# Laying the operand tiles of a decoder layer at one address residue, and cutting the key and value columns at 256

## The chip, the cores and the metric

The kernel runs on one core of a Trainium2 chip. The metric is the device time of one execution in microseconds; less is better. Its operands are float32; most matrix products are made from a high and a low part of each operand, in three matmuls (high by high, high by low, low by high).

## The reference

One decoder layer over 1024 tokens of width 1024 (batch 1), cut to its lines of computation:

```python
mod = silu(c) @ ada_w + ada_b                       # six rows: shift, scale, gate, twice
u = rms_norm(h, norm1_g) * (1 + scale1) + shift1
z = u @ w_in                                        # queries, keys, values, gates, 2 x 1024 merge columns
y_a = nsa_attention(...) @ w_up_nsa                 # compressed, selected and window branches, 8 heads
y_b = stick_breaking_attention(q_b, k_b, v_b) @ w_up_sb
mixed = (sigmoid(m_a) * y_a + sigmoid(m_b) * y_b) @ w_out
h = h + gate1 * mixed
u2 = rms_norm(h, norm2_g) * (1 + scale2) + shift2
h = h + gate2 * (square(relu(u2 @ mlp_w1)) @ mlp_w2)    # 4096 hidden columns
```

## The kernel before

The program is one straight list of work in stages. The times are those of the profiled execution.

- 0 to 185 us: normalisation, modulation, the first projections. `block_mm` (L302, L306) and `q_mm` (L577) make queries and the sources of the compressed blocks; `kv_mm` (L588) makes keys, values and gates for each of 8 token tiles, in two groups of 24 matmuls, over columns 0 to 272 and 272 to 536.
- to 600 us: `nsa_all`, the sparse attention. Logits are two matmuls a chunk (L825, L826: query tile `qh` or `ql` as weights, `kT` streamed); the probabilities are turned (L943) and multiplied with the values (L909: `vS` as weights, `th` or `tl` streamed). In between, `drive` and `pump` put 1,344 matmuls of `unit_mm` (L746) that project the remaining 28 blocks of 128 columns of `w_in` (weights `uwh`, `uwl`; `uh`, `ul` streamed, 512 columns each).
- to 880 us: `sb_gens`, the stick-breaking attention, with the rest of `unit_mm` in between.
- to 975 us: `up_unit`, 16 units for each of two branches, 12 matmuls a unit (L1324: weights `wh`, `wl`; the attention outputs `oh`, `ol` streamed). Branch 0 runs three units ahead: the first three units are of branch 0 alone, then the branches alternate, and the last three are of branch 1 alone.
- to 1105 us: `out_mm`, 16 units of 24 matmuls (L1428: `mth`, `mtl` as weights, `wh` or `wl` streamed), and the second normalisation with its turns (L1447).
- to the end: the channel mixer in 8 chunks of 512 hidden columns. `hidden_units` is 8 units a chunk of 24 matmuls (L1512: `wh`, `wl` as weights, `mth`, `mtl` streamed, which by then hold `u2`); `product` is 7 products a chunk of 24 matmuls (L1561: `rah`, `ral` as weights, `wbh`, `wbl` streamed). One unit and one product take turns, until the last chunk, whose seven products have no further units beside them.

"Weights" is the 128 x 128 operand that TensorE loads, "streamed" the operand of up to 512 columns that runs past it; the loading of the next weights overlaps the running matmul.

Tiles come from two stacks of pools that grow from either end of the on-chip memory, "left" from below and "right" from above. A pool's place is what the pools opened before it leave. Each tile takes its size rounded up to 32 bytes, so that a pool with odd-sized tiles shifts all that is opened after it. What is given below as a residue is a tile's start within a partition, modulo 512 bytes, as the built program has it:

| pool (side) | tiles | before | after |
|---|---|---|---|
| uT, wu, mt, ml (left) | uh, ul, uwh, uwl, mth, mtl, rah, ral, wbh, wbl | 128 | 128 |
| p1a (left) | wh1, wl1 (2176 bytes each, 8 buffers) | 0, 128, 256, 384 | the same |
| xt (right) | xT, xa, ch1, cl1 | 448 | 128 |
| kv (right) | kT, vS, kcT | 192 | 128 |
| at (right) | qh, ql | 384 | 128 |
| at (right) | Sn, Pn, Pf | 128 | 128 |
| at (right) | th, tl | 448 | 128 |
| sb (right) | Q, Kh, Kl, V | 64 | 128 |
| sb (right) | th, tl, sigr | 448 | 128 |
| wr, wx, wq (right) | raw, wh, wl | 448 | 128 |
| ya (right) | oh, ol of branch 0 | 448 | 128 |
| yb (left) | oh, ol of branch 1 | 128 | 128 |

A weight or streamed slice starts at its tile's residue plus a multiple of 512, but for the slices of `wh1` and `wl1` in `kv_mm`: the first group starts at the tile's residue, the second 272 x 4 = 1088 bytes behind it, which is 64 more modulo 128.

Of the kernel before, what the change touches and what calls it, by code (L numbers as in the profile page):

```python
# [6 lines left out]
F32 = mybir.dt.float32  # L7
# [10 lines left out]
NT = 8  # L18
# [17 lines left out]
def build(tc, I, out):  # L36
# [89 lines left out]
    pre_l = pre.tile([128, NK, 128], F32R, name="uwl")  # L126
    p1a = pool("p1a", "left")

    pool("odd", "right").tile([128, 8], F32, name="odd")
    xt_pool = pool("xt", "right")  # L130


# [263 lines left out]
    kvp = pool("kv", "right")  # L396
    kT = kvp.tile([128, 4, S], F32R, name="kT")
    vS = kvp.tile([128, NT, 4, 2, HD], F32R, name="vS")
    kcT = kvp.tile([128, 2, HD], F32R, name="kcT")
    gates = kvp.tile([128, NT, 8, 3], F32, name="gates")  # L400
    vC = kvp.tile([HD, 2, 2, HD], F32R, name="vC")
    bnp = pool("bn", "right")
    Bn = bnp.tile([128, 8, 256], F32, name="Bn")
# [177 lines left out]

    def kv_mm(t):
        raw = pb.tile([128, 544], F32, name="kvr", bufs=2)
        for c, (c0, c1) in enumerate(((0, 272), (272, 536))):
            p = (pd, psx)[c]()
            for k in range(NK):
                for n, (a, b) in enumerate(three(k, slice(t * 128, (t + 1) * 128))):
                    nc.tensor.matmul(p[:, :c1 - c0], a, ws[k][b][:, c0:c1],  # L588
                                     start=(k == 0 and n == 0), stop=(k == NK - 1 and n == 2))
            nc.scalar.copy(raw[:, c0:c1], p[:, :c1 - c0])  # L590
        return raw
# [59 lines left out]
    for n, (kind, t) in enumerate(jobs):  # L651
# [8 lines left out]
        if kind == "q":  # L660
            b = q_mm(t)
# [6 lines left out]
        else:  # L668
            if t == 0:
                ws = wk  # L670
            b = kv_mm(t)
# [86 lines left out]
    at = pool("at", "right")  # L758
# [43 lines left out]

    PT_ = 0.216


    def nsa_a(i, kv, hp, qT, P):
        n0, n1 = max(0, i - 1), i + 1
        x0 = 256 - (n1 - n0) * 128
        nb = 8 * i + 8
        chunks = plan(i)  # L810
        ngm = at.tile([128, 2, 2, 3], F32, name="ngm", bufs=2)
        sms = at.tile([128, 2, 2, 3], F32, name="sms", bufs=2)
        if len(chunks) < 6:
            nc.vector.memset(ngm, 3e38)
            nc.vector.memset(sms, 0.0)
        late = None
        for g in range(2):
            h = kv * 4 + hp * 2 + g
            q0, q1 = qT[0][:, hp * 2 + g], qT[1][:, hp * 2 + g]
            for br, c, a, b in chunks:  # L820
                n = (b - a) * 128
                p = psx()
                em = br == 1 and c == 1 and i >= 4
                kk = kT[:, br * 2 + kv, a * 128:b * 128]
                track(nc.tensor.matmul(p[:, :n], q0, kk, start=True, stop=False))  # L825
                track(nc.tensor.matmul(p[:, :n], q1, kk, start=False, stop=not em))  # L826
                if em:
                    track(nc.tensor.matmul(p[:, :128], identr, edger, start=False, stop=True))
                nm = ngm[:, br, g, c:c + 1]
                sm = sms[:, br, g, c:c + 1]  # L830
                if c == 0:
                    src = at.tile([128, 256], F32, name="Sn", bufs=3)
                    nc.vector.tensor_tensor_reduce(src[:, :n], p[:, :n], Bn[:, h, x0:], -1.0, 3e38,
                                                   op0=OP.add, op1=OP.min, accum_out=nm)
                    dst = at.tile([128, 256], F32, name="Pn", bufs=8)
                else:
                    src = p
                    nc.vector.tensor_reduce(nm, p[:, :n], axis=AX.X, op=OP.max, negate=True)
                    dst = at.tile([128, 384], F32, name="Pf", bufs=12)
                P[br, g, c] = dst  # L840
                if late:
                    late()

                def late(src=src, dst=dst, n=n, c=c, nm=nm, sm=sm):
                    nc.scalar.activation(dst[:, :n], src[:, :n], AF.Exp, scale=-1.0 if c == 0 else 1.0,
                                         bias=nm, accum_out=sm)
                yield max(n, 256) * 2 / 2400.

        p = psx()
        for g in range(2):  # L850
            for q in range(2):
                track(nc.tensor.matmul(p[:, g * 64:g * 64 + nb], qT[q][:, hp * 2 + g], kcT[:, kv, :nb],
                                 start=q == 0, stop=q == 1))
        late()
        sc = at.tile([128, 2, HD], F32, name="sc", bufs=2)
        nc.vector.tensor_tensor(sc[:, :, :nb], p[:, :128].rearrange("p (g c) -> p g c", g=2)[:, :, :nb],
                                Bc[:, kv * 4 + hp * 2:kv * 4 + hp * 2 + 2, 56 - 8 * i:56 - 8 * i + nb], op=OP.add)
        mc = at.tile([128, 2], F32, name="mc", bufs=2)
        nc.vector.tensor_reduce(mc, sc[:, :, :nb], axis=AX.X, op=OP.max, negate=True)
        nc.vector.scalar_tensor_tensor(sc[:, :, :nb], mc[:, :, None].to_broadcast([128, 2, nb]), 1e20, sc[:, :, :nb],  # L860
                                       op0=OP.min, op1=OP.add)
        pcx = at.tile([128, 2, HD], F32, name="pcx", bufs=2)
        P["c"] = pcx

        mm = at.tile([128, 2, 2], F32, name="mm", bufs=2)
        nc.vector.tensor_reduce(mm, ngm, axis=AX.X, op=OP.min)
        fc = at.tile([128, 2, 2, 3], F32, name="fc", bufs=2)
        nc.vector.tensor_tensor(fc, mm[:, :, :, None].to_broadcast([128, 2, 2, 3]), ngm, op=OP.subtract)
        yield 0.43
        nc.scalar.activation(pcx[:, :, :nb], sc[:, :, :nb], AF.Exp)  # L870
        nc.scalar.activation(fc, fc, AF.Exp)
        yield 0.0
        tot = at.tile([128, 3, 2], F32, name="tot", bufs=2)
        nc.vector.tensor_reduce(tot[:, 0], pcx[:, :, :nb], axis=AX.X, op=OP.add)
        nc.vector.tensor_tensor(sms, sms, fc, op=OP.mult)
        nc.vector.tensor_reduce(tot[:, 1:3], sms, axis=AX.X, op=OP.add)
        nc.vector.tensor_scalar(tot, tot, 1e-30, None, op0=OP.max)
        nc.vector.reciprocal(tot, tot)
        h0 = kv * 4 + hp * 2
        nc.vector.tensor_tensor(tot, tot, gates[:, i, h0:h0 + 2].rearrange("p g s -> p s g"), op=OP.mult)  # L880
        nc.vector.tensor_tensor(fc, fc, tot[:, 1:3][:, :, :, None].to_broadcast([128, 2, 2, 3]), op=OP.mult)
        nc.gpsimd.tensor_tensor(pcx[:, :, :nb], pcx[:, :, :nb], tot[:, 0][:, :, None].to_broadcast([128, 2, nb]), op=OP.mult)
        P["fc"] = fc
        yield 0.0


    def nsa_b(i, kv, hp, P):
# [42 lines left out]
        for n in range(len(items) + 2):  # L930
# [3 lines left out]
            if n <= last:  # L934
                it = items[n]
                p = pt()
# [17 lines left out]
            yield cost  # L954
        tmp = at.tile([64, 256], F32, name="otmp", bufs=2)
        nc.scalar.copy(tmp, po_[64:128, :256])
        o = at.tile([64, 256], F32, name="osum", bufs=2)
        nc.vector.tensor_tensor(o, po_[0:64, :256], tmp, op=OP.add)
        h0 = (kv * 4 + hp * 2) * HD
        nc.sync.dma_start(oa_d[h0:h0 + 128, i * 128:(i + 1) * 128].rearrange("(g d) q -> d g q", g=2),  # L960
# [93 lines left out]


    def sb_gens(sp):
        zero = sp.tile([128, 16], F32, name="zero")[:, 0:1]
        nc.vector.memset(zero, 0.0)

        def load(u, h):  # L1060
# [54 lines left out]
        def sb_a(kind, chunk, ops, A, edges):  # L1115

            i, c0, c1 = chunk
            Q, Kh, Kl = ops
            w = c1 - c0
            p = psx()  # L1120
            qs = Q[:, i * 128:(i + 1) * 128]
            diag = kind != 2
            track(nc.tensor.matmul(p[:, :w], qs, Kh[:, c0:c1], start=True, stop=False))
            track(nc.tensor.matmul(p[:, :w], qs, Kl[:, c0:c1], start=False, stop=not diag))
            if diag:
                track(nc.tensor.matmul(p[:, w - 128:w], identr, diagr, start=False, stop=True))
            sig = sp.tile([128, w], F32, name="sigr" if kind == 1 else "sig%d" % w, bufs=5 if kind == 1 else 2)
            nc.scalar.activation(sig, p[:, :w], AF.Sigmoid, scale=HD ** -0.5)
            nc.scalar.activation(p[:, :w], p[:, :w], AF.Sigmoid, scale=-(HD ** -0.5))
            A[i, kind] = (sig, c0)  # L1130

            def fin():
                Pt = sp.tile([128, 528], F32, name="Pt", bufs=6)
                if diag:
                    nc.vector.memset(Pt[:, w:w + 1], 1.0)
                else:
                    nc.vector.tensor_copy(Pt[:, w:w + 1], edges.pop(i)[:, 0:1])
                nc.vector.tensor_tensor_scan(Pt[:, 0:w][:, ::-1], p[:, 0:w][:, ::-1], zero.to_broadcast([128, w]),
                                             1.0 if diag else Pt[:, w:w + 1], op0=OP.mult, op1=OP.add)
                nc.gpsimd.tensor_tensor(sig, sig, Pt[:, 1:w + 1], op=OP.mult)  # L1140
                if kind == 1:
                    edges[i] = Pt
            return fin, max(w, 256) * 2 / 2400.
# [469 lines left out]
```

## Time and profile before

| | |
|---|---|
| median of three runs | 1754.13 us (1746.5 to 1754.78) |
| the profiled execution | 1753.26 us |
| its span, first to last instruction | 1751.5 us |
| TensorE (PE) busy | 1694.7 us, 97% |
| weight loads (PEld) | 1414.9 us, 81% |
| VectorE (DVE) | 1141.8 us, 65% |
| ScalarE (ACT) | 819.8 us, 47% |
| GpSimd (POOL) | 876.1 us, 50% |
| mean granted clock of TensorE | 0.989 |

The profile is of one execution. A busy share says how long some instruction of an engine was under way; matmuls overlap each other (one that is shown with 0.39 us may start 0.23 us after the one before), so the pace of TensorE is read from the starts, not from the durations.

### The profile page before, as it was taken

To read this page: it belongs to the slowest core of one execution; us is meant where nothing else is said; L and a number is where in the kernel's file an instruction comes from. 1 tells how busy PE (TensorE), PEld (TensorE's weight loads), DVE (VectorE), ACT (ScalarE), POOL (GpSimd) and SP (SyncE) were. 2 spreads that over 40 slices of the span, in tenths; PEclk is the share of its full clock that TensorE was granted. 3 is DMA by queue.
4 is the path that set the end of the run, shared out by engine and by line. 5 is a ranking of instruction groups with operands and counts; after the bars stand their busy time and mean duration, and the time that the engine had idled before them with its cause. 6 is when DMAs were issued, how large, how long until landed. Compare 5 with 4: busy or idle time off the path is not lost.

```text
span 1751.5 us, 25194 instructions
## 1 busy us (share of the span) xinstructions
PE 1694.7 (97%) x8652; PEld 1414.9 (81%) x8652; DVE 1141.8 (65%) x2514; ACT 819.8 (47%) x1809; POOL 876.1 (50%) x824
## 2 busy tenths in 40 slices
PE   5999999999999989999999899999999999999998
PEld 4879888888888867788778688888888888888886
DVE  7597478778777567878464564365656575756458
ACT  6433476666666466766433244333333333333332
POOL 0021143434333387865164400786857675858676
PEclk8999999999999989999999999999999999999999
DMA  9365311111121264531485611121212020202102
GB/s 304 97 185 160 109 46 55 55 54 54 49 61 38 62 167 124 157 88 46 135 256 183 216 37 73 38 71 37 70 39 73 25 73 25 72 25 72 41 21 97
DMA packets 153656, 157.14 MB, mean 90 GB/s; under 512 B 13544, under 2 KB 117688, under 8 KB 153528
## 3 DMA queue, kind: packets, MB, share of 16 engines
q1 hardware_dynamic: 149304, 153.42, 29.3%
q10 hardware_dynamic: 4224, 2.10, 0.4%
q8 instruction: 69, 1.13, 0.3%
q14 instruction: 59, 0.48, 0.1%
HBM read 128.21 MB, written 27.28 MB: 89 GB/s over the span
## 4 chain that ended last, share of the span: by engine, by line
PE 83%; DMA 5%; DVE 4%; POOL 3%; ACT 3%; issue 2%; SPq 1%; POOLq 0%; DVEq 0%; ACTq 0%
PE px L1512 20%; PE px L1561 16%; PE pd L746 15%; PE px L1428 5%; PE po L909 4%; PE pt L943 4%; PE px L1324 3%; DMA adraw<-in_ada_w_dram 2%; PE psx L825 2%; PE psx L826 2%; PE cb L302 1%; PE pd L588 1%; PE po L1175 1%; PE psx L588 1%; PE pt L1155 1%
## 5 line engine op out<-in xcount | busy, mean ns | idle before, releaser
L1564 DVE TENSOR_TENSOR acc<-acc,px 128x512 f32<-128x512 f32 x384 | 243.9, 683 | 119.8 <-PE px L1561 114.5
L1512 PE MATMUL px<-mtl,wh 128*128 128x512 f32 x512 | 202.9, 396 | 0.0
L1512 PE MATMUL px<-mth,wl 128*128 128x512 f32 x512 | 202.7, 396 | 0.0
L1512 PE MATMUL px<-mth,wh 128*128 128x512 f32 x512 | 202.5, 396 | 0.0
L746 PE MATMUL pd<-uh,uwh 128*128 128x512 f32 x448 | 181.3, 405 | 0.7 <-ACT zo L1018 0.7
L1561 PE MATMUL px<-wbl,rah 128*128 128x512 f32 x448 | 175.3, 391 | 2.2 <-POOL wbl L1537 1.9
L746 PE MATMUL pd<-ul,uwh 128*128 128x512 f32 x448 | 177.1, 395 | 0.0
L746 PE MATMUL pd<-uh,uwl 128*128 128x512 f32 x448 | 177.1, 395 | 0.0
L1561 PE MATMUL px<-wbh,ral 128*128 128x512 f32 x448 | 174.9, 390 | 0.0
L66 DVE TENSOR_TENSOR wl<-raw,wh 128x1024 fp32r<-128x1024 f32 x48 | 76.3, 1591 | 149.1 <-ACT wh L61 128.7
L1561 PE MATMUL px<-wbh,rah 128*128 128x512 f32 x448 | 172.1, 389 | 0.0
L1537 POOL TENSOR_TENSOR wbl<-raw,wbh 128x1024 fp32r<-128x1024 f32 x40 | 106.0, 2649 | 91.9 <-ACT wbh L1536 91.6
L1523 POOL TENSOR_TENSOR w<-w,grow 128x1024 f32<-128x1024 f32 x32 | 82.8, 2602 | 97.0 <-DVE grow L1296 96.4
L901 DVE TENSOR_TENSOR tl<-pt,th 128x512 fp32r<-128x512 f32 (+8 forms) x168 | 103.7, 620 | 34.3 <-ACT th L900 33.0
L1535 POOL TENSOR_TENSOR raw<-r 128x512 f32<-128x512 f32 x80 | 109.9, 1397 | 20.0 <-DVE wl L66 17.9
L900 ACT CAST th<-pt 128x512 fp32r<-128x512 f32 (+8 forms) x168 | 88.8, 531 | 60.6 <-PE pt L943 58.0
L1512 PEld LDWEIGHTS px<-mth,wl 128*128 128x128 f32 x512 | 96.2, 188 | 23.6 <-issue 0.5
L1512 PEld LDWEIGHTS px<-mtl,wh 128*128 128x128 f32 x512 | 96.3, 188 | 23.0 <-issue 0.2
L1512 PEld LDWEIGHTS px<-mth,wh 128*128 128x128 f32 x512 | 96.2, 188 | 22.9 <-issue 0.2
L1536 ACT CAST rah<-raw 128x1024 fp32r<-128x1024 f32 x40 | 42.1, 1052 | 153.1 <-PE px L1561 139.7
L1561 PEld LDWEIGHTS px<-wbl,rah 128*128 128x128 f32 x448 | 84.1, 188 | 22.1 <-POOL wbl L1537 3.1
L746 PEld LDWEIGHTS pd<-uh,uwl 128*128 128x128 f32 x448 | 84.7, 189 | 18.1
(322 smaller groups left out, 4548.3 us busy)
## 6 DMA issues: line engine op xcount, KB each, us to landing
raw<-in_mlp_w_dram SPq DMA_DIRECT2D x32, 512.0 KB, 4.0
w<-in_mlp_w_dram SPq DMA_DIRECT2D x32, 512.0 KB, 4.0
z_d<-zo SPq DMA_DIRECT2D x56, 256.0 KB, 2.2
uwr<-in_w_in_dram SPq DMA_DIRECT2D x54, 256.0 KB, 3.0
adraw<-in_ada_w_dram SPq DMA_DIRECT2D x48, 256.0 KB, 2.9
xa<-in_ada_w_dram SPq DMA_DIRECT2D x32, 256.0 KB, 6.1
zr<-z_d SPq DMA_DIRECT2D x32, 256.0 KB, 4.8
m<-z_d SPq DMA_DIRECT2D x32, 256.0 KB, 3.6
```

The costliest lines, as they stand in the source:

```text
L66: (nc.vector if e == "v" else nc.gpsimd).tensor_tensor(dst, src, f(h), op=OP.subtract)
L746: r = nc.tensor.matmul(p, a, b, start=(k == 0 and n == 0), stop=(k == NK - 1 and n == 2))
L900: nc.scalar.copy(th[:rows, :w], p[:rows, :w])
L901: nc.vector.tensor_tensor(tl[:rows, :w], p[:rows, :w], f(th)[:rows, :w], op=OP.subtract)
L909: track(nc.tensor.matmul(po_[:, :256], w, tt[q][:rows, m * 256:(m + 1) * 256], start=(n == 0 and m == 0 and q == 0), stop=(n == last and m ...
L1428: nc.tensor.matmul(p, a[:, k, ts_], b[:, k % 2], start=(k == 0 and n == 0), stop=(k == NK - 1 and n == 2))
L1512: nc.tensor.matmul(p, a[:, k], b[th][:, k], start=(k == 0 and m == 0), stop=(k == NK - 1 and m == 2))
L1523: nc.gpsimd.tensor_tensor(t, t, grow2, op=OP.mult)
L1535: nc.gpsimd.tensor_tensor(d, block(i0, j0, s), block(i1, j1, s), op=OP.add if sg > 0 else OP.subtract)
L1537: (nc.vector if e == "v" else nc.gpsimd).tensor_tensor(l.rearrange("p s n -> p (s n)"), src, f(h).rearrange("p s n -> p (s n)"), op=OP.sub ...
L1561: nc.tensor.matmul(p, a[:, s, qs], b[:, s], start=(s == 0 and n == 0), stop=(s == 1 and n == 2))
L1564: nc.vector.tensor_tensor(acc[:, t, ds_], acc[:, t, ds_], p, op=OP.add if sg > 0 else OP.subtract)
```

## The change

Six paddings. The tile `odd`, which nothing reads, grows from 8 to 88 columns and so moves everything on the right by 320 bytes. `gates` (768 bytes) takes 1024. The small tiles of `nsa_a` (48, 24, 16 or 8 bytes) take 256 bytes each; `osum` takes 1152 for 1024; `zero` takes 512 for 64; `Pt` 2560 for 2112. And `kv_mm` cuts its 536 columns at 256 instead of 272.

```diff
-    pool("odd", "right").tile([128, 8], F32, name="odd")
+    pool("odd", "right").tile([128, 88], F32, name="odd")
...
-    gates = kvp.tile([128, NT, 8, 3], F32, name="gates")
+    gates = kvp.tile([128, 256], F32, name="gates")[:, :NT * 24].rearrange("p (t h s) -> p t h s", t=NT, h=8)
...
-        for c, (c0, c1) in enumerate(((0, 272), (272, 536))):
+        for c, (c0, c1) in enumerate(((0, 256), (256, 536))):
...
+    def small(name, n=12):
+        return at.tile([128, 64], F32, name=name, bufs=2)[:, :n]
...
-        ngm = at.tile([128, 2, 2, 3], F32, name="ngm", bufs=2)
-        sms = at.tile([128, 2, 2, 3], F32, name="sms", bufs=2)
+        ngm, sms = (small(n).rearrange("p (b g c) -> p b g c", b=2, g=2) for n in ("ngm", "sms"))
...
-        mc = at.tile([128, 2], F32, name="mc", bufs=2)
+        mc = small("mc", 2)
...
-        mm = at.tile([128, 2, 2], F32, name="mm", bufs=2)
+        mm = small("mm", 4).rearrange("p (b g) -> p b g", b=2)
...
-        fc = at.tile([128, 2, 2, 3], F32, name="fc", bufs=2)
+        fc = small("fc").rearrange("p (b g c) -> p b g c", b=2, g=2)
...
-        tot = at.tile([128, 3, 2], F32, name="tot", bufs=2)
+        tot = small("tot", 6).rearrange("p (b g) -> p b g", b=3)
...
-        o = at.tile([64, 256], F32, name="osum", bufs=2)
+
+        o = at.tile([64, 288], F32, name="osum", bufs=2)[:, :256]
...
-        zero = sp.tile([128, 16], F32, name="zero")[:, 0:1]
+        zero = sp.tile([128, 128], F32, name="zero")[:, 0:1]
...
-                Pt = sp.tile([128, 528], F32, name="Pt", bufs=6)
+                Pt = sp.tile([128, 640], F32, name="Pt", bufs=6)
```

The order of the instructions stays as it was on POOL and SP; on PE, DVE and ACT a few neighbours in the stretch of `kv_mm` and of the compressed blocks change places. On PE, in the first keys and values tile, these rows stand before (`wh` and `wl` are the weights' high and low columns of `w_in`, numbered by buffer; `uh`, `ul` the tokens; `pd` and `psx` the two output banks):

```order
L588 MATMUL pd<-wh_1128,uh 128x272
L588 MATMUL pd<-wl_1129,uh 128x272
L588 MATMUL pd<-wh_1128,ul 128x272
L588 MATMUL psx<-wh_1116,uh 128x264
L588 MATMUL psx<-wl_1117,uh 128x264
L588 MATMUL pd<-wh_1134,uh 128x272
```

and these in their place now:

```order
L588 MATMUL pd<-wh_1128,uh 128x256
L588 MATMUL pd<-wl_1129,uh 128x256
L588 MATMUL pd<-wh_1128,ul 128x256
L588 MATMUL psx<-wh_1116,uh 128x280
L588 MATMUL psx<-wl_1117,uh 128x280
L588 MATMUL pd<-wh_1134,uh 128x256
```

The number of matmuls and the sum of the columns are the same; 16 columns have moved from the first group to the second.

Where a new pool is laid over an old one, what its tiles wait for follows their addresses. On SP's queue, at the start of `up_unit`, the loads of the attention outputs (`raw`) and of the merge columns (`m`) stand before as

```order
L1309 DMA raw<-oa_d 128x1024 [waits DMAHW3_49,Pool_49]
L1329 DMA m_11387<-z_d 128x512 [waits DMAHW4_49]
L1329 DMA m_11559<-z_d 128x512 [waits DMAHW5_49,PE_49]
L1329 DMA m_11580<-z_d 128x512 [waits DMAHW6_49]
L1329 DMA m_11607<-z_d 128x512 [waits DMAHW7_49]
```

and now as

```order
L1312 DMA raw<-oa_d 128x1024 [waits DMAHW3_49,Pool_49]
L1332 DMA m_11387<-z_d 128x512 [waits DMAHW4_49]
L1332 DMA m_11559<-z_d 128x512 [waits DMAHW5_49]
L1332 DMA m_11580<-z_d 128x512 [waits DMAHW6_49,PE_49]
L1332 DMA m_11607<-z_d 128x512 [waits DMAHW7_49]
```

The wait for TensorE has moved from the second load of `m` to the third. On the new kernel's lines all numbers behind L802 are 2 or 3 higher: L1512 is L1515 there, L1561 is L1564, L1324 is L1327, L1428 is L1431.

## Rows read from the trace of the kernel before

**Rows 1.** The page's chain that ended last, by line.
```profile
PE px L1512 20%; PE px L1561 16%; PE pd L746 15%; PE px L1428 5%; PE po L909 4%; PE pt L943 4%; PE px L1324 3%; DMA adraw<-in_ada_w_dram 2%; PE psx L825 2%; PE psx L826 2%; PE cb L302 1%; PE pd L588 1%; PE po L1175 1%; PE psx L588 1%; PE pt L1155 1%
```
**Rows 2.** Busy us by stage: window, its length, engines' busy (instructions), clock, DMA.
```profile
160.00:600.00 440.00, 436.49 (x2808) 386.97 (x2806) 323.08 (x1172) 268.79 (x820) 157.07 (x318) 1.00 0.21 58
600.00:880.00 280.00, 262.14 (x1370) 216.72 (x1369) 193.01 (x363) 173.15 (x387) 166.60 (x171) 0.98 0.43 120
880.00:990.00 110.00, 103.50 (x452) 83.41 (x451) 58.81 (x68) 40.81 (x64) 60.33 (x42) 0.97 0.61 196
990.00:1105.00 115.00, 114.55 (x529) 93.44 (x528) 59.07 (x109) 47.48 (x119) 5.25 (x5) 1.00 0.28 101
1105.00:1751.50 646.50, 640.59 (x2773) 520.24 (x2771) 390.06 (x482) 214.78 (x290) 469.74 (x264) 1.00 0.17 52
```
**Rows 3.** Page's groups: count, busy us, mean ns, idle before and its releaser.
```profile
L1512 PE MATMUL px<-mtl,wh 128*128 128x512 f32 x512 | 202.9, 396 | 0.0
...
L1561 PE MATMUL px<-wbl,rah 128*128 128x512 f32 x448 | 175.3, 391 | 2.2 <-POOL wbl L1537 1.9
```
**Rows 4.** Timeline of PE in the last chunk: start us, duration us, line, operands.
```profile
1704.42 0.39 PE L1512 MATMUL px<-mth,wl 128*128 128x512 f32 x1
...
1706.05 0.39 PE L1561 MATMUL px<-wbh,rah 128*128 128x512 f32 x1
...
1707.44 0.39 PE L1561 MATMUL px<-wbh,rah 128*128 128x512 f32 x1
...
1716.96 1.07 PE L1561 MATMUL px<-wbh,rah 128*128 128x512 f32 x4
```
**Rows 5.** Timeline of PE, L1324 while branch 0 runs alone.
```profile
883.57 0.39 PE L1324 MATMUL px<-oh,wh 128*128 128x512 f32 x1
...
887.42 0.39 PE L1324 MATMUL px<-ol,wh 128*128 128x512 f32 x1
```
**Rows 6.** Timeline of PE, L1324 while branch 1 runs alone.
```profile
966.03 0.39 PE L1324 MATMUL px<-oh,wl 128*128 128x512 f32 x1
...
973.03 0.40 PE L1324 MATMUL px<-oh,wl 128*128 128x512 f32 x1
```
**Rows 7.** Timeline of PE, a stretch of L1428.
```profile
1059.62 0.39 PE L1428 MATMUL px<-wh,mth 128*128 128x512 f32 x1
...
1063.98 0.40 PE L1428 MATMUL px<-wl,mth 128*128 128x512 f32 x1
```
**Rows 8.** Timeline of PE, L746 alone, near the end of its work.
```profile
860.18 0.39 PE L746 MATMUL pd<-uh,uwh 128*128 128x512 f32 x1
...
865.85 0.39 PE L746 MATMUL pd<-ul,uwh 128*128 128x512 f32 x1
```
**Rows 9.** Timeline of PE in the sparse attention.
```profile
404.70 0.28 PE L825 MATMUL psx<-kT,qh 128*128 128x256 f32 x1
...
405.41 0.28 PE L909 MATMUL po<-th,vS 128*128 128x256 f32 x1
...
405.87 0.28 PE L909 MATMUL po<-th,vS 128*128 128x256 f32 x1
...
406.58 0.40 PE L746 MATMUL pd<-uh,uwh 128*128 128x512 f32 x1
...
407.98 0.17 PE L852 MATMUL psx<-kcT,qh 128*128 128x16 f32 x1
```
**Rows 10.** Timeline of PE in keys and values.
```profile
121.12 0.29 PE L588 MATMUL pd<-wl,uh 128*128 128x272 f32 x1
...
122.12 0.28 PE L588 MATMUL psx<-wh,uh 128*128 128x264 f32 x1
...
124.09 0.28 PE L588 MATMUL psx<-wh,ul 128*128 128x264 f32 x1
...
124.93 0.28 PE L588 MATMUL psx<-wh,uh 128*128 128x264 f32 x1
```
**Rows 11.** The page's DMA issues: line, count, KB each, median us to landing.
```profile
m<-z_d SPq DMA_DIRECT2D x32, 256.0 KB, 3.6
```

## The prediction

> **What bounds the kernel now.** First the chain that ended last: matmul lines hold it, L1512 with 20%, L1561 with 16%, L746 with 15% [rows 1]. Then the stages: in the channel mixer TensorE is busy 640.6 of 646.5 us, in the sparse attention 436.5 of 440, in the output projection 114.6 of 115; only the stick-breaking stage (262 of 280) and the up projections (103.5 of 110) leave it idle, and the clock is 0.97 or more in all five [rows 2]. L1512 has no idle time before it, L1561 2.2 us in all [rows 3]. So the kernel goes at the pace of its matmuls, and a busy share cannot show whether that pace is the best there is. That needs the third view, the starts in the timeline.
>
> **The pace of a 512-column matmul differs by line.** In the last chunk one window holds three paces [rows 4]. L1512 runs 7 intervals from 1704.42 to 1706.05: 233 ns each. Then L1561 takes over, 6 intervals to 1707.44: 232 ns. Then 42 intervals to 1716.96, across the start of the next product: 9.52 / 42 = 226.7 ns. Shape, stage and clock are the same. What differs in the table of residues: L1561 streams and loads at 128; L1512 streams at 128 and loads weights at 448, which is 64 off modulo 128.
>
> The cleanest pair is in L1324, one line of code run for two branches. Branch 0 alone (both operands at 448) makes 17 intervals from 883.57 to 887.42: 226.5 ns [rows 5]. Branch 1 alone (streams at 128, weights at 448) makes 30 from 966.03 to 973.03: 233.3 ns [rows 6]. So neither residue is slow; the pair is, when the two differ by 64 modulo 128. L746, both at 128, makes 25 intervals from 860.18 to 865.85: 226.8 ns [rows 8]. L1428, streaming at 448 with weights at 128, is between: 19 intervals from 1059.62 to 1063.98, 229.5 ns [rows 7]. I read it as the running matmul and the load of the next weights getting in each other's way in the on-chip memory.
>
> A rule speaks against this. The Trainium skill ("TensorE: Matmul & The Clock Gate", Part 2, first step) says that TensorE has two independent read ports and that loading the next weights takes no read bandwidth from the running matmul; "SBUF — State Buffer", Who interferes with whom, has it that TensorE waits for nobody. By it no residue could matter and the sum would be 0. The trace does not agree: 226.5 against 233.3 ns for one line.
>
> **The change part by part.** After it all of L1512, L1324, L1428 and L746 stream and load at 128.
>
> - L1512: 512 matmuls of each of three kinds [rows 3], 1,536. Each goes from 233.0 to 226.7 ns [rows 4]: 6.3 ns, 9.7 us. TensorE never waits there, so all of it counts.
> - The six slow intervals of L1561 behind L1512 cost 6 x (231.7 - 226.7) = 30 ns. The product that follows a product has none: the 42 even intervals run across its start [rows 4]. So they are the way back from L1512's pace. L1512 stands ahead of 50 of the 56 products (7 in each of the first seven chunks, the first of the last): 1.5 us.
> - L1324: the 192 matmuls of branch 1 gain 6.8 ns, 1.3 us; branch 0 loses its ways back after each unit of branch 1, about 13 units at 30 ns, 0.4. Some may sink into the 6.5 us of idle time there [rows 2]. I take 1.5.
> - L1428: 384 by 229.5 - 226.7: 1.1 us; the turns in between break its runs, so 0.9.
> - L302 (96 matmuls, weights `ch1` at 448 over tokens at 128): the trace has no even run of it. From 0 to 96 x 6.8 = 0.65; I take 0.3.
> - L746 keeps its residues, but in the attention it comes in runs of a few: 406.58 to 407.98 is 6 intervals of 233 ns, behind other shapes [rows 9]. If those are ways back that even residues cure, up to all 1,344 matmuls gain 6.5 ns, 8.7 us; if they come from the change of shape, 0. L909 ahead of that run was already even (448 and 448), so I take it near the low end: 0.5.
> - Shorter matmuls. L825 and L826 (192 and 384, odd by 64) make 6 intervals of 256 columns from 404.70 to 405.41, L909 (448 and 448) 6 from 405.87 to 406.58: 118 ns both [rows 9]. Evening them gives nothing. In keys and values the even group (272 columns) makes 8 intervals in 1.00 us, 125 ns, and the odd one (264) 7 in 0.84, 120 [rows 10]. Eight columns at 226.7 / 512 = 0.44 ns are 3.5 ns; so the odd group is 1.5 ns the better. The 16 columns moved cancel, and evening the second group costs 0 to 192 x 1.5 = 0.3 us; the same 1.5 on L825 and L826, 248 of each by the chunks of `plan`, would be 0.7. I take 0.5 lost.
> - DVE, ACT and POOL only get other addresses. L1512 and L1561 wait for them 2.2 us in all [rows 3], so a few ns on one of their instructions lie beside matmuls. The moved wait at the start of the up projections: before, the third load of `m` stood behind the second, which waited for TensorE; now it waits itself, one load later in the same queue. Behind it stand the fourth load and the first weights. Cost 0; without cover, one landing of 3.6 us [rows 11].
>
> Sum: 9.7 + 1.5 + 1.5 + 0.9 + 0.3 + 0.5 - 0.5 = 13.9 us. Against the profiled execution, 1753.3 (span 1751.5 and 1.8 around it), that gives **1739.4 us**. The median shown is 0.9 above that execution, less than the spread of the three runs, so I leave it at 1739.5.
>
> **The rivals.**
>
> - *Half the effect.* The pace may depend on the distance of the two operands more finely than by 64 modulo 128: L1428's pair is odd too and costs only 2.8 ns. If L1512 settles at L1428's 229.5 [rows 7], it gains 3.5 x 1,536 = 5.4 us, the ways back stay, and the rest gives about 1.5: **1746.5**. Against it: branch 0, L1561 and L746, at distances that are all multiples of 512, show 226.5 to 226.8.
> - *It is not the residue.* In the slow pairs the streamed tile is also on the left of the memory and the weights on the right; in branch 0 both are on the right, in L1561 and L746 both on the left. If it is the side, the change moves nothing across and the time is **1753**, or 0.5 above. Against it: L1428 crosses sides as well and is less slow. The skill's rule on ports, above, ends at the same time.
> - *Slower: other engines come in the way.* In the attention stages TensorE, DVE, ACT and POOL would all work on tiles at 128. If an access of theirs holds up a matmul as an odd pair does, the place is L746 between 185 and 850 us. At 6.5 ns on 1,344 matmuls that is 8.7 us lost, and the time 1748; slower than before it is from 13.9 / 1,344 = 10.3 ns each, slower by 0.5% from 17 ns: **1763**. Against it: in the mixer L1561 holds 226.7 ns [rows 4] while POOL is busy 470 of 646 us and DVE 390 [rows 2], mostly on tiles at 128.
>
> **How the numbers follow.** 0.5% of the median, 8.8 us, is about what a measurement here can tell from no change; the border is 1745.4. Forecast, 0.72: from 1731 (all of L746's 8.7 us) to 1745. Half effect, 0.12, on both sides of the border. Not the residue, 0.12, within 0.5%. Other engines, 0.04. So faster 0.72 + 0.06 = 0.78, the same 0.18, slower 0.04. The range 1731 to 1750 takes in the forecast and the half effect and leaves out the last two.
>
> **What would show it.** Right: the starts of the mixer's hidden units at 226.7 ns with no slow six behind them, the up projections of both branches at one pace, the mixer's stage shorter by 11 us, the idle times as before. L746 in short runs tells the open term: 233 ns still, or 227. Wrong: hidden units still at 233 (the side), at 229 (the distance), or L746 above 233 in the attention stages (other engines).

## The result, and the profile after

| | before | after |
|---|---|---|
| median of six runs | 1754.65 us (1746.5 to 1756.73) | 1739.42 us (1735.5 to 1743.83) |
| after / before, 95% interval | | 0.992 (0.9901 to 0.9938) |
| the profiled execution, its span | 1753.26, 1751.5 us | 1738.83, 1736.9 us |

The kernel is 0.8% faster, 10.9 to 17.4 us by the interval; 1739.5 us was forecast. A second comparison on another chip, with 6 runs of the change, gave 0.9923 (0.9907 to 0.9939):

> The changed kernel unaltered, timed beside the next one: 1739 us.

It took 1737.95 us beside 1751.8.

The page of the changed kernel first: the chain by line, then groups as in [rows 3] and the loads as in [rows 11]. L1515 was L1512, L1564 was L1561, L1327 was L1324, L1431 was L1428.

```profile
PE px L1515 20%; PE px L1564 16%; PE pd L746 16%; PE px L1431 5%; PE po L911 4%; PE pt L945 4%; PE px L1327 3%; DMA adraw<-in_ada_w_dram 2%; PE psx L827 2%; PE psx L828 2%; PE po L1178 1%; PE cb L302 1%; PE psx L588 1%; PE pd L588 1%; PE pt L1158 1%
...
L1515 PE MATMUL px<-mtl,wh 128*128 128x512 f32 x512 | 199.6, 390 | 0.0
...
L1564 PE MATMUL px<-wbl,rah 128*128 128x512 f32 x448 | 174.8, 390 | 2.1 <-POOL wbl L1540 1.8
...
m<-z_d SPq DMA_DIRECT2D x32, 256.0 KB, 3.6
```

The chain is the same one as in [rows 1]. One matmul of the hidden units is shown with 390 ns where it had 396, those of the products with 390 where they had 391, and the idle times before them are as they were. The loads of `m` land as fast as before, and the first three, of which the third now waits for TensorE, are issued within 1.4 us where it was 1.5; the moved wait cost nothing there.

The pace is in the starts. TensorE's timeline (start us, duration us, line, operands): a short run of L746 in the sparse attention, as in [rows 9], the up projections while branch 1 runs alone, as in [rows 6], and the last chunk, as in [rows 4]:

```profile
404.30 0.40 PE L746 MATMUL pd<-uh,uwh 128*128 128x512 f32 x1
...
405.69 0.17 PE L854 MATMUL psx<-kcT,qh 128*128 128x16 f32 x1
...
963.62 0.39 PE L1327 MATMUL px<-oh,wl 128*128 128x512 f32 x1
...
969.06 0.39 PE L1327 MATMUL px<-oh,wl 128*128 128x512 f32 x1
...
1689.99 0.39 PE L1515 MATMUL px<-mth,wl 128*128 128x512 f32 x1
...
1691.58 0.39 PE L1564 MATMUL px<-wbh,rah 128*128 128x512 f32 x1
...
1692.94 0.39 PE L1564 MATMUL px<-wbh,rah 128*128 128x512 f32 x1
...
1702.46 1.07 PE L1564 MATMUL px<-wbh,rah 128*128 128x512 f32 x4
```

From the bottom up: the 7 intervals of the hidden unit take 1.59 us, 227 ns each, where they had 233. The first 6 of the product take 1.36 us, 227 ns, where they had 232, and the 42 behind them 226.7 as before: one pace is left. Branch 1 makes 24 intervals in 5.44 us, 226.7 ns, where it had 233.3. L746 makes 6 intervals in 1.39 us, 232 ns: the short run is as slow as it was.

Where the time came from is seen by cutting each trace at three starts: the first up projection, the first hidden unit and the last matmul of the last product. The kernels e1 to e6 are those of the next section. "Even" is a kernel whose hidden units stream and load at the same residue, "odd" one where they are 64 off.

| | start to up projections | from there to the hidden units | from there to the last product | TensorE's wait at the start of the out projection |
|---|---|---|---|---|
| before (odd) | 879.2 | 197.2 | 670.9 | 4.9 |
| e2 (odd) | 877.7 | 197.3 | 672.0 | 3.7 |
| after (even) | 876.9 | 196.3 | 659.5 | 6.2 |
| e5, the same again (even) | 880.8 | 195.9 | 659.6 | 5.8 |
| e1 (even) | 878.9 | 196.4 | 659.6 | 6.8 |
| e3 (even) | 878.6 | 195.5 | 659.6 | 5.4 |
| e6 (even) | 875.5 | 196.7 | 659.6 | 6.4 |

All times are in us. The mixer takes 659.5 to 659.6 us in every even trace, 11.3 to 11.4 less than before. The up and out projections together give 0.5 to 1.7 against the trace of before. The last column is one wait for the weights `wh`, which POOL (L63) makes; in the profiled pair, the first row from the trace of before:

```profile
PE px L1428 <- POOL wh L63: 4.9, 1, 4.9
...
PE px L1431 <- POOL wh L63: 6.2, 1, 6.2
```

These are the total, the number of waits and the longest. The stretch before the up projections differs by 4 us between executions of one kernel (876.9 and 880.8), so that the 2.3 us that the profiled pair shows there say nothing.

### The profile page after: what moved, and what is told of

It reads as the page before. It is cut to its first block, busy times and chain, and to the rows that moved or that the text cites. A ratio compares the mean times of both kernels' runs of the same rounds, so it can differ in the third digit from the quotient of the medians.

```text
span 1736.9 us, 25196 instructions
## 1 busy us (share of the span) xinstructions
PE 1680.8 (97%) x8652; PEld 1415.5 (81%) x8652; DVE 1143.5 (66%) x2514; ACT 818.7 (47%) x1809; POOL 871.7 (50%) x824
## 4 chain that ended last, share of the span: by engine, by line
PE 83%; DVE 5%; DMA 4%; ACT 3%; POOL 3%; issue 2%; SPq 0%; POOLq 0%; DVEq 0%; ACTq 0%
PE px L1515 20%; PE px L1564 16%; PE pd L746 16%; PE px L1431 5%; PE po L911 4%; PE pt L945 4%; PE px L1327 3%; DMA adraw<-in_ada_w_dram 2%; PE psx L827 2%; PE psx L828 2%; PE po L1178 1%; PE cb L302 1%; PE psx L588 1%; PE pd L588 1%; PE pt L1158 1%
## 5 line engine op out<-in xcount | busy, mean ns | idle before, releaser
L1515 PE MATMUL px<-mtl,wh 128*128 128x512 f32 x512 | 199.6, 390 | 0.0
L1515 PE MATMUL px<-mth,wl 128*128 128x512 f32 x512 | 199.4, 390 | 0.0
L1515 PE MATMUL px<-mth,wh 128*128 128x512 f32 x512 | 199.2, 389 | 0.0
L746 PE MATMUL pd<-uh,uwh 128*128 128x512 f32 x448 | 181.5, 405 | 0.7 <-ACT zo L1021 0.7
L746 PE MATMUL pd<-ul,uwh 128*128 128x512 f32 x448 | 178.2, 398 | 0.0
L746 PE MATMUL pd<-uh,uwl 128*128 128x512 f32 x448 | 177.2, 396 | 0.0
L1564 PE MATMUL px<-wbl,rah 128*128 128x512 f32 x448 | 174.8, 390 | 2.1 <-POOL wbl L1540 1.8
L1564 PE MATMUL px<-wbh,ral 128*128 128x512 f32 x448 | 174.3, 389 | 0.0
L1564 PE MATMUL px<-wbh,rah 128*128 128x512 f32 x448 | 171.9, 389 | 0.0
L1515 PEld LDWEIGHTS px<-mth,wl 128*128 128x128 f32 x512 | 96.1, 188 | 20.5 <-DVE grow L1299 0.2
L1515 PEld LDWEIGHTS px<-mth,wh 128*128 128x128 f32 x512 | 96.1, 188 | 20.1 <-issue 0.2
L1515 PEld LDWEIGHTS px<-mtl,wh 128*128 128x128 f32 x512 | 96.1, 188 | 20.1 <-issue 0.2
L1564 PEld LDWEIGHTS px<-wbl,rah 128*128 128x128 f32 x448 | 84.1, 188 | 21.2 <-POOL wbl L1540 3.1
L746 PEld LDWEIGHTS pd<-uh,uwl 128*128 128x128 f32 x448 | 85.1, 190 | 17.8
```

What stands on the lines that cost most here:

```text
L746: r = nc.tensor.matmul(p, a, b, start=(k == 0 and n == 0), stop=(k == NK - 1 and n == 2))
L1515: nc.tensor.matmul(p, a[:, k], b[th][:, k], start=(k == 0 and m == 0), stop=(k == NK - 1 and m == 2))
L1564: nc.tensor.matmul(p, a[:, s, qs], b[:, s], start=(s == 0 and n == 0), stop=(s == 1 and n == 2))
```

## The experiments

**e1: the one tile alone.** The kernel before, with nothing else:

```diff
-    pool("odd", "right").tile([128, 8], F32, name="odd")
+    pool("odd", "right").tile([128, 88], F32, name="odd")
```

> The kernel before with one edit: the unused tile grows from 8 to 88 columns, so that all pools on the right start 320 bytes lower. The weights of the hidden units, the up projections and the output projection then lie at 128 like the streamed tiles; the attention tiles stay odd, the other five paddings and the cut at 256 are left out. Theory of the residue (streamed operand and next weights 64 apart modulo 128 cost 6 ns a matmul): hidden units at 226.7 ns, 1754.6 - 13.5 = 1741 us, within 2 us of the whole change. Rival, the side of the memory: hidden units still at 233 ns, 1754 us. Rival, the attention's tiles bring the gain: 1748 or more.

Measured: 1737.64 us beside 1752.67, ratio 0.9905 (0.9887 to 0.9923). The page's group of the hidden units:

```profile
L1512 PE MATMUL px<-mtl,wh 128*128 128x512 f32 x512 | 199.6, 390 | 0.0
```

This is the row of the changed kernel to the digit. One padding of 320 bytes on a tile that nothing reads gives the whole gain; the other paddings and the cut at 256 give nothing that can be measured.

**e2: the changed kernel, with the right side 64 bytes off.**

```diff
-    pool("odd", "right").tile([128, 88], F32, name="odd")
+    pool("odd", "right").tile([128, 72], F32, name="odd")
```

> The changed kernel with the unused tile at 72 columns in place of 88: everything on the right lies 64 bytes higher, at 192 modulo 512; everything else is as changed. Theory of the residue: the hidden units' weights are 64 off again (192 against 128), 233 ns a matmul, all of the gain in the mixer is lost, 1752 to 1755 us. Rival, a finer dependence on the distance: 64 need not cost what 320 cost before, 1743 to 1748. Rival, what counts is the padding of the small tiles: 1739 as the changed kernel.

Measured: 1752.3 us beside 1752.67, ratio 0.9993 (0.9981 to 1.0006). The group has the 396 ns of [rows 3] again:

```profile
L1515 PE MATMUL px<-mtl,wh 128*128 128x512 f32 x512 | 202.9, 396 | 0.0
```

and the timeline of the last hidden unit the pace of [rows 4]:

```profile
1699.71 0.39 PE L1515 MATMUL px<-mth,wh 128*128 128x512 f32 x1
...
1704.38 0.39 PE L1515 MATMUL px<-mth,wl 128*128 128x512 f32 x1
```

20 intervals in 4.67 us, 233.5 ns. With every other part of the change in place, 64 bytes take the whole gain back.

**e3: both sides 64 off.** As e2, and the left side lifted too:

```diff
+    pool("lift", "left").tile([128, 16], F32, name="lift")
...
-    pool("odd", "right").tile([128, 88], F32, name="odd")
+    pool("odd", "right").tile([128, 72], F32, name="odd")
```

> The changed kernel with both sides at 192 modulo 512: the unused tile on the right at 72 columns, and a new unused tile of 16 columns on the left ahead of the token tiles. All pairs are even, but no tile starts at a multiple of 128. Theory of the residue of the pair: hidden units 226.7 ns, products 226.7 ns, 1739 us. Rival, each tile must start at a multiple of 128 by itself: hidden units and products at 230 ns or more, 1750 us or more.

Measured: 1739.72 us in one execution, the mixer 659.6 us. Residue 128 has no merit of its own; what matters is the distance between the two operands.

**e4: the pace over the distance.** A kernel of nothing but matmuls: the same streamed tile, and weights from 32 tiles, 16 on the left (`neara` to `nearp`, the first at the streamed tile's residue) and 16 on the right (`fara` to `farp`), each 32 bytes further modulo 512; 48 matmuls of each with 512 columns, then with 256.

```diff
+    near = [wp.tile([128, 1032], F32R, name="near" + c) for c in letters]
+    far = [hp.tile([128, 1032], F32R, name="far" + c) for c in letters]
...
+            nc.tensor.matmul(p[:, :cols], t[:, m % 8 * 128:(m % 8 + 1) * 128],
+                             xs[:, m % 4 * 512:m % 4 * 512 + cols], start=m == 0, stop=m == n - 1)
```

> No layer is computed: 48 matmuls each with one streamed tile (at a fixed residue on the left) and, in turn, 16 weight tiles on the left and 16 on the right, each 32 bytes further modulo 512 than the one before; first with 512 columns, then with 256. Theory of the residue: left and right alike; with 512 columns 226.7 ns where the distance is 0, 128, 256 or 384 modulo 512, and about 233 where it is 64, 192, 320 or 448; 32-byte steps are open. With 256 columns 118 ns at all distances. Rival, the side: 227 ns for all on the left, 233 for all on the right. Rival, a finer dependence: a different pace at each distance.

Its timeline, one row for each tile; the pace is the next row's start less this one's, by 48:

```profile
17.41 11.35 PE L61 MATMUL bka<-str,nearb 128*128 128x512 f32 x48
28.60 11.36 PE L61 MATMUL bka<-str,nearc 128*128 128x512 f32 x48
39.80 11.40 PE L61 MATMUL bka<-str,neard 128*128 128x512 f32 x48
51.03 11.32 PE L61 MATMUL bka<-str,neare 128*128 128x512 f32 x48
62.19 11.37 PE L61 MATMUL bka<-str,nearf 128*128 128x512 f32 x48
73.39 11.16 PE L61 MATMUL bka<-str,nearg 128*128 128x512 f32 x48
84.39 11.36 PE L61 MATMUL bka<-str,nearh 128*128 128x512 f32 x48
95.58 11.05 PE L61 MATMUL bka<-str,neari 128*128 128x512 f32 x48
106.47 11.35 PE L61 MATMUL bka<-str,nearj 128*128 128x512 f32 x48
...
240.44 11.05 PE L61 MATMUL bka<-str,farf 128*128 128x512 f32 x48
251.33 11.35 PE L61 MATMUL bka<-str,farg 128*128 128x512 f32 x48
...
362.79 5.92 PE L61 MATMUL bka<-str,neara 128*128 128x256 f32 x48
368.54 5.84 PE L61 MATMUL bka<-str,nearb 128*128 128x256 f32 x48
374.22 5.82 PE L61 MATMUL bka<-str,nearc 128*128 128x256 f32 x48
379.87 5.79 PE L61 MATMUL bka<-str,neard 128*128 128x256 f32 x48
```

| weights less streamed, modulo 256 | 0 | 32 | 64 | 96 | 128 | 160 | 192 | 224 |
|---|---|---|---|---|---|---|---|---|
| 512 columns, ns (tiles `neari`, then `nearb` to `nearh`) | 226.9 | 233.1 | 233.3 | 234.0 | 232.5 | 233.3 | 229.2 | 233.1 |
| 256 columns, ns (tiles `neara` to `nearh`) | 119.8 | 118.3 | 117.7 | 117.5 | 118.5 | 119.6 | 117.9 | 117.9 |

The row repeats every 256 bytes, and left and right give the same (`neari` and `farf`, both at 0, 10.89 us). So it is not the side. It is not "64 modulo 128" either: 128 is as slow as 64, and 192, the pair of L1428 in [rows 7], is a value of its own at 229. With 256 columns distance 0 is among the slowest. The first row of this trace, `neara` with 512 columns, is not used: its first matmuls came 427 ns apart.

**e8: the right side 128 off.** The changed kernel, with `odd` of 56 columns. The weights are then 128 from the streamed tile: by the prediction's rule (only 64 modulo 128 costs) that is a fast distance, by the table a slow one.

```diff
-    pool("odd", "right").tile([128, 88], F32, name="odd")
+    pool("odd", "right").tile([128, 56], F32, name="odd")
```

> The changed kernel with the unused tile at 56 columns: everything on the right at 256 modulo 512, so that the hidden units' weights are 128 from the streamed tiles. By the prediction's rule (64 modulo 128 is what costs) 226.7 ns and 1739 us; by the sweep, whose paces repeat every 256 bytes, 232.4 ns, and about 1751 us.

Its group:

```profile
L1515 PE MATMUL px<-mtl,wh 128*128 128x512 f32 x512 | 202.4, 395 | 0.0
```

395 ns, and 669.4 us from the first hidden unit to the last product, where even kernels have 659.6. The period is 256 in the kernel too. Its time, 1745.7 us in one execution, lies between the others because its part ahead of the up projections took only 873.2 us; the mixer is what tells the theories apart.

**e9: 16-byte steps.** As e4, with distances 0 to 240 modulo 256 in steps of 16 (`neara` to `nearp`), and 512 and 384 columns.

> As the first sweep (no layer is computed; 48 matmuls for each weight tile), but all weight tiles on the left and their distance to the streamed tile in steps of 16 bytes from 0 to 240; with 512 columns, then with 384. If the pace follows the distance modulo 256 alone, the even steps repeat the first sweep (226.7, 233.4, 233.4, 234.3, 232.4, 233.4, 228.8, 233.3) and the odd ones lie between 227 and 235; whether another distance than 0 reaches 226.7 is open. With 384 columns about 171 to 177.

```profile
18.37 11.05 PE L61 MATMUL bka<-str,nearb 128*128 128x512 f32 x48
29.25 11.35 PE L61 MATMUL bka<-str,nearc 128*128 128x512 f32 x48
40.45 11.36 PE L61 MATMUL bka<-str,neard 128*128 128x512 f32 x48
...
129.99 11.20 PE L61 MATMUL bka<-str,nearl 128*128 128x512 f32 x48
141.03 11.15 PE L61 MATMUL bka<-str,nearm 128*128 128x512 f32 x48
152.02 11.36 PE L61 MATMUL bka<-str,nearn 128*128 128x512 f32 x48
...
174.41 11.06 PE L61 MATMUL bka<-str,nearp 128*128 128x512 f32 x48
185.31 8.51 PE L61 MATMUL bka<-str,neara 128*128 128x384 f32 x48
...
260.51 8.68 PE L61 MATMUL bka<-str,nearj 128*128 128x384 f32 x48
269.02 8.64 PE L61 MATMUL bka<-str,neark 128*128 128x384 f32 x48
```

At 16 and at 240 bytes the pace is still 227 ns (10.88 and 10.90 us for 48), at 32 it is 233 (11.20). At 176 and 192 it is 230 and 229. With 384 columns the steady pace is 173.3 ns at most distances, 32 to 64 among them, and at the worst, 144, 177 (8.51 us for 48). Which distances are slow depends on the number of columns.

**e7: only the low weights odd.** The changed kernel, with `wl` of the hidden units 64 bytes off and `wh` even; one matmul in three, (mth, wl), loads odd weights, and the one ahead of it, (mtl, wh), runs while they are loaded.

```diff
-        wh, wl = ((pool_ or L["wr"]).tile([128, D], F32R, name=name, bufs=n) for name in ("wh", "wl"))
+        wh = (pool_ or L["wr"]).tile([128, D], F32R, name="wh", bufs=n)
+        wl = pool_.tile([128, D], F32R, name="wl", bufs=n) if pool_ else L["wr"].tile([128, D + 64], F32R, name="wl", bufs=n)[:, 16:16 + D]
```

> The changed kernel, but in the weight pool of the hidden units the low part wl alone starts 64 bytes later; the high part wh and the streamed tiles stay at 128. The three matmuls of a step are wh over mth, wh over mtl, wl over mth; while the second runs, wl is loaded. Theory that the load of the next weights meets the streamed read: only the second of the three is slow (its load is the odd one), mean about 229 ns. Rival, a matmul is slow by its own weights: the third is. If both are, or all, the order of the reads shifts from one matmul to the next. Mean 228 to 230, total 1742 to 1745 us.

Its lines view of the hidden units (count: duration ns min/median/max, first and last start us):

```profile
L1516 PE MATMUL px<-mth,wh x512: 389/389/476, 1073.3 to 1697.9; 128*128 128x512 f32 x171
...
L1516 PE MATMUL px<-mtl,wh x512: 388/392/796, 1073.7 to 1698.1; 128*128 128x512 f32 x171
...
L1516 PE MATMUL px<-mth,wl x512: 389/397/794, 1073.9 to 1698.4; 128*128 128x512 f32 x171
```

From its start to the next one, (mth, wl) takes 235.7 ns in the mean of the units' steady part, (mtl, wh) 229.2 and (mth, wh) 228.4; all three have 226.7 in the changed kernel. The loads stand in the same timeline as PEld:

```profile
1695.35 0.39 PE L1516 MATMUL px<-mtl,wh 128*128 128x512 f32 x1
1695.36 0.19 PEld L1516 LDWEIGHTS px<-mth,wl 128*128 128x128 f32 x1
1695.58 0.40 PE L1516 MATMUL px<-mth,wl 128*128 128x512 f32 x1
...
1695.82 0.39 PE L1516 MATMUL px<-mth,wh 128*128 128x512 f32 x1
```

The load of `wl` begins and ends inside the 0.23 us of (mtl, wh); the 0.24 us come behind it. The mixer is 666.4 us, 6.9 more than in the changed kernel, and the one execution took 1745.92 us, a little above the 1742 to 1745 expected, as the mean of the three, 231.1 ns, is above the 228 to 230. The matmul that is held up most is the one whose own weights are odd, not the one that runs while they are loaded.

**e6: the attention's pairs at 64.** By e4 the 256-column matmuls of the attention would like a distance of 64 better than 0. `odd` of 88 columns and the other sizes of before, with a tile that shifts part of the pool `at`, put its pairs there:

```diff
+    shift = []
...
+            if not shift:
+                shift.append(at.tile([128, 16], F32, name="shift"))
...
-        o = at.tile([64, 288], F32, name="osum", bufs=2)[:, :256]
+        o = at.tile([64, 264], F32, name="osum", bufs=2)[:, :256]
```

> The kernel before with the unused tile at 88 columns, and two paddings of 64 bytes in the attention pool (a tile of 16 columns ahead of th, osum at 264 columns): weights and streamed tile of the two logit matmuls and of the value matmuls then lie 64 apart modulo 256, those of the 512-column products 0 apart; small tiles, Pt, zero, gates and the cut at 272 as before. From the sweep, 256 columns cost 117.8 ns at a distance of 64 and 120.0 at 0. Theory: value matmuls (592) and logits (496) save about 2 ns each against the changed kernel, 2 us, 1737 us; the mixer as in the changed kernel. Rival, the sweep's steady runs do not carry over to the attention's runs of a few: 1739 us, and the spacing there stays at 120.

Measured: 1737.6 us, ratio to before 0.992 (0.9907 to 0.9933), against 0.9923 (0.9907 to 0.9939) for the changed kernel beside it (e5). Against that kernel (lines by the numbers of before) L909's interval with `tl` went from 119.0 to 117.9 ns, L826's from 119.2 to 118.2, L909's with `th` from 118.0 to 118.6. The steady difference of 2 ns does not arrive in full in short runs; no version beat the changed kernel by what can be measured.

**e10: does the shape bring the way back?** The even tile `neara` (distance 0) in runs of 16 matmuls of 512 columns (L71), each behind 6 others (L68): with 256 columns and even, with 256 and at 64, with 512 and at 64, and with 512, even, from another tile. "The way back" is the prediction's name for the slow intervals before the even pace holds.

```diff
+            for m in range(n_short):
+                nc.tensor.matmul(q[:, :cols], short[:, m % 8 * 128:(m % 8 + 1) * 128],
+                                 xs[:, m % 4 * 512:m % 4 * 512 + cols], start=m == 0, stop=m == n_short - 1)
+            for m in range(n_long):
+                nc.tensor.matmul(p, near[0][:, m % 8 * 128:(m % 8 + 1) * 128],
+                                 xs[:, m % 4 * 512:m % 4 * 512 + 512], start=m == 0, stop=m == n_long - 1)
```

> No layer is computed. Runs of 16 matmuls of 512 columns at distance 0, each behind 6 others: of 256 columns at distance 0, of 256 columns at distance 64, of 512 columns at distance 64, and of 512 columns at distance 0 with another tile. Theory of the way back: behind 6 odd matmuls of 512 columns about six slow intervals (230 to 236), then 226.7; behind even ones of the same shape none. For the attention's short runs: if a change of shape alone calls for a way back, the runs behind 256 columns start slow at both distances; if only an odd pair does, the run behind 256 columns at distance 0 starts at 226.7.

Its timeline, one round of the first, the third and the fourth kind:

```profile
19.20 3.82 PE L71 MATMUL bka<-str,neara 128*128 128x512 f32 x16
22.85 0.88 PE L68 MATMUL bkb<-str,neara 128*128 128x256 f32 x6
...
151.42 3.82 PE L71 MATMUL bka<-str,neara 128*128 128x512 f32 x16
155.07 1.56 PE L68 MATMUL bkb<-str,nearc 128*128 128x512 f32 x6
...
227.82 3.79 PE L71 MATMUL bka<-str,neara 128*128 128x512 f32 x16
231.44 1.52 PE L68 MATMUL bkb<-str,neari 128*128 128x512 f32 x6
```

The 16 take 3.65 us behind matmuls of 256 columns, be they even or at 64, 3.65 behind odd ones of 512, and 3.62 behind even ones of 512. In the first case the starts go 233, 236, 228, 233, 231 and then 227 ns: 27 ns over five intervals. So a change of shape brings the way back even when every operand is even. Whether a slow distance does so depends on the distance: in e4 `neari` and `farf` follow tiles at 224, which go at 233 ns, and their first interval is 227 already.

## Why the prediction was right, point by point

- **The step that carried it**, hidden units from 233.0 to 226.7 ns, came as said. By the sums of start-to-start intervals L1515 took 350.03 us for 359.91: 9.9 us, forecast 9.7.
- **The slow six behind the hidden units** are gone: L1564 took 1.5 us less, forecast 1.5. The mixer as a whole gave 11.4 us, forecast 11.2.
- **L1324** gave 1.7 us by the same sums (90.64 to 88.97), forecast 1.5, and both branches go at one pace. Most of it did not reach the end of the stage, as the next point shows.
- **L1428** was forecast to give 0.9 and gave nothing: its steady pace went to 227 ns, but the sum went from 96.31 to 97.09 us. The step that failed is that faster matmuls in these two stages shorten them; the prediction let only 0.2 us of L1324's gain sink into idle time. Near its start L1428 waits once for `wh` of L63, which POOL makes; this wait grew from 4.9 us to 6.2. The five even traces of the table have 5.4 to 6.8, the two odd ones 4.9 and 3.7. Without the wait the sum fell by 0.5 us (91.4 to 90.9). The up projections gain, the weights arrive when they did (the matmul that waits for them starts 105.4 us behind the first up projection before and 105.1 after), and most of that gain turns into waiting. Of the 2.4 us forecast for the two stages 0.5 to 1.7 arrived.
- **L746**, 0.5 with bounds of 0 and 8.7: the value is 0. Its sum went from 323.80 to 324.86 us, and 323.36 in the second profile of the same kernel. e10 shows why: behind shorter matmuls a run of 6 ends as its way back does. The prediction's sign for this, L909 ahead of the run being even, holds but not as it reads the table: `th` is at 448 and `vS` at 192, 256 apart and not at one residue.
- **Short matmuls**, 0.5 lost: L825 and L826 together lost 0.3 us (73.42 to 73.70), the direction that e4 has for distances 192 and 0. The prediction read 118 ns for both stretches of [rows 9] from starts rounded to 10 ns; unrounded they are 117.8 and 119.3, which is that difference. Keys and values gave 0.04 us (51.36 to 51.32). L302, 0.3 forecast, went from 25.84 to 25.54 us, and 26.68 in the second profile of the changed kernel: no gain can be told.
- **Three of the rivals fell.** The side of the memory: e2 and e3, which move nothing across, and e4. Other engines: the mixer's pace holds with POOL and DVE at work, and L746's short run makes 232 ns, no more than before. The sum of 0 by the rule of the Trainium skill ("TensorE: Matmul & The Clock Gate", Part 2, first step, and "SBUF — State Buffer", Who interferes with whom), by which TensorE reads its operands independently and waits for nobody: e1 differs from the kernel before, and e2 from e3, by addresses alone, and by 15.0 and 12.6 us. That the load takes nothing from the running matmul is not refuted by this: e7 finds most of the loss in another matmul.
- **The rival "finer than 64 modulo 128" was right about the form and wrong about the time.** The pace does depend on the distance more finely, with a period of 256, but the change puts the pair at 0, which is the best place by either rule. That the forecast came out rests on this, and here the prediction had luck. L1428 at 192 and L1512 at 64 are equal modulo 128 and go at 229 and 233 ns, so that the trace of before already spoke against a period of 128; what it lacked was a steady run of 512 columns at 128, which a kernel like e8 would have met. The change leaves such pairs: half of the tiles `wh1` and `wl1` (residues 0 and 256) stay 128 from the tokens, and no run moves them.
- **The total** came out better than its parts. 1739.4 us were measured for 1739.5, but the traces show 11.4 us in the mixer and 0.5 to 1.7 in the two stages ahead of it, 12 to 13 for the 13.9 forecast, and executions of the changed kernel lie between 1735.5 and 1743.8. The agreement to 0.1 us is luck.
- **The reading that the next weights' load gets in the way** fell with e7. What in the chip ties the pace of a running matmul to the address from which its weights have already been read stays open.

## What to carry to other kernels

When TensorE is busy throughout, compare the starts of matmuls of one shape line by line; two steady paces at one clock suggest that the faster can be had everywhere. For float32 operands with 512 columns and new weights for each matmul, lay the start of the weights and that of the streamed operand at a distance of a multiple of 256 bytes, within 16: one padding at the head of a pool can do it, and it was worth 0.8% here. Do it for long runs of one shape; runs of about six behind matmuls of 256 columns stayed slow at distance 0 too.

## What was not expected of the hardware

- The pace of 512-column matmuls over the distance has a period of 256 bytes, with one good place (226.7 ns within 16 bytes of 0), one middling (230 and 229 at 176 and 192) and 232 to 234 elsewhere.
- For 256 columns the good place is among the bad ones: 119.8 ns at 0, 117.5 at 96. For 384 it is 173.3 at most distances and up to 177.
- After a change of shape from 256 to 512 columns, or after matmuls at a distance of 64, the pace comes back over five to six matmuls, at a cost of 27 to 30 ns in all, while a change of tile alone costs nothing, and behind matmuls at a distance of 224 there is nothing to come back from.
- Faster matmuls in the up projections turned into 0.5 to 3.1 us more of waiting for weights at one place, as the table of the first section shows.
